# Half of a_u by seven block products, with the bias chain, the dot products and the softmax factor moved, in a decoder block kernel

## The chip, the cores and the metric

The kernel runs on one core of a Trainium2 chip, as one launch. The time is device microseconds of that core: 792.88 us in the median of three runs (792.55 to 793.46). The traces are those of one profiled execution.

## The reference

One decoder layer over x of 512 tokens x 1024 channels, in float32, then a final RMSNorm. Cut to what the change touches:

```
h   = rms_norm(x, norm1_g) * (1 + scale1) + shift1      # shifts, scales, gates: silu(c) @ w_ada + b_ada
z   = h @ w_in        # a_u 1024 | a_v 1024 | q 1024 | k 256 | v 256 | qi 512 | ki 64 | wi 8 | g_a 1024 | g_b 1024
v'  = layer_norm(gelu(a_v), gmlp_ln_g, gmlp_ln_b)       # in 4 chunks of 128 positions and 8 groups of 128 channels
y_a = gelu(a_u) * (einsum('gts,nsgc->ntgc', tril(w_s), v') + b_s)
score  = sum over 8 indexer heads of wi * relu(qi . ki / 8), causal; each query keeps its 128 best keys
y_b    = softmax attention (8 heads of 128, 2 key heads, partial rotary) over the kept keys
merged = sigmoid(g_a) * (y_a @ w_proj_a) + sigmoid(g_b) * (y_b @ w_proj_b)
x = x + gate1 * (merged @ w_out);  x = x + gate2 * swiglu_ffn(rms_norm(x) modulated)
```

Each of the six modulation sections (1024 values) is 8 dot products of 128 rows of the transposed `w_ada` with silu(c).

## The kernel before

Every product with more than float32r precision is made of three matmuls: the weights and the activations are each split into a float32r high part `hi` and the remainder `lo`, and hi*hi, hi*lo and lo*hi are added in PSUM (`mm3`, lines 65 to 68). The order of all instructions is written out by hand; each engine runs its own in program order and waits only on data and on buffers that come free.

**The weight stream.** All weights and most rows of `w_ada` come in one list, `stream`, in fixed order. An entry is 512 KB: a weight chunk ("w") or one dot product ("m"). `issue` (line 91) allocates its raw buffer and puts its load on SyncE's queue. `prep` (line 118) uses it up: a weight chunk gets its `hi` on ScalarE (line 134) and its `lo` on VectorE or GpSimd (line 138); a dot product is one VectorE instruction over the whole 128x1024 raw tile (line 209). A chunk is asked for by `get(i, ahead=2)`, which prepares the stream, in order, up to the weight chunk two behind; before each preparation it issues what has room. The plain raw buffers are three (`RAWB = 3`, line 73):

```
    def room(i):
        ...
        return sum(p["kind"] == "w" or not (p["early"] or p["mid"]) for p in pend) < RAWB
```

Here `pend` is what lies between the entry to be prepared next and entry i. Dot products that are marked "mid" have a tile of their own instead (a tag such as "acc" or "A2") and do not count. `group` (line 231) adds a group of 256 output columns as two chunks of four 128-row blocks, with `nm` dot products behind each chunk.

**The stages around the change.** Indexer and query projections come first, then a_v in eight chunks (steps `vs` 0 to 7, tasks in `VT`), beside which the indexer's scores are built (`idx_mm`, `idx_acc`). Then a_u: four groups, two chunks each (`opt_b`, steps 0 to 7 of `au_tasks` and `au_post`), each chunk 24 matmuls of 512 columns, and behind each chunk a dot product through the tile "acc". In the same steps run the layer norm of v', the spatial mixing (`mix_mm(m)` and `mix_ev(m)` at the steps of `AT`), the bias (`rs_mm`: two matmuls with a tile of ones give the row sums of the masked `w_s`; `bias_mix`: eight VectorE instructions), and the top-k search over the scores, two VectorE passes per round, at the counts of `BG`. Then gate A in two rounds of 512 columns (`xround`, line 1095), each followed by two groups of `w_proj_a` (steps to 29).

**Seven products.** `xround` computes a 512x512 block of columns as a 2x2 block product with seven products instead of eight. One product is 24 matmuls of 256 columns. Sums of weight blocks are formed in DRAM by copying and adding transfers on GpSimd's queue (`x_moves`, eight transfers per round, issued one by one by `x_move`); sums of the activations (`h_sum`, `h_hi`, `h_lo`) are made once and kept.

**Attention with gate B.** `for s in range(NU + 3)` (line 1260) runs 16 attention units in steps; one unit is 128 queries of two heads. Step s does, in this order: the product with v of unit s-3 (`at_pv`) and its evacuation; the scores of unit s (`at_qk`) and their masked maximum on VectorE (`at_soft_a`); the transposes of unit s-2 with `th` on ScalarE and `tl` on VectorE; the softmax factor of unit s-1 (`at_soft_b`, VectorE); the query split of unit s+2 (`qh` ScalarE, `ql` VectorE); the exponentials of unit s (`at_exp`, ScalarE); and `gb_part`, one or two of the 32 pieces of gate B (12 matmuls of 512 columns a pair of column tiles), by

```
    GBN = [1, 2, 2, 1, 1, 1, 2, 2, 2, 2, 2, 2, 2, 2, 2, 2, 2, 2, 0]
```

`gb_part` calls `get` for its chunk, with ahead 1 in step 0 and 2 from then on, so step 1 prepares the stream up to the first chunk of gate B's group 1, and step 2 up to the second. Behind each of gate B's eight chunks stands one dot product, in a plain raw buffer (`nm=1, mraw=False`, line 284). The `lo` of group 1's first chunk is on VectorE, that of its second on GpSimd.

Of the kernel before, what the change touches and what calls it, by code (L numbers as in the profile page):

```python
# [28 lines left out]
def block_kernel(ctx: ExitStack, tc: tile.TileContext, x, x_t, c_row, positions, w_ada_t, w_first, w_in, w_blocks,  # L29
                 gmlp_w_s, gmlp_b_s, w_proj_a, w_proj_b,  # L30
# [868 lines left out]
    def mask_ws():  # L899
        P.affine_select(late["wmT"], late["wmT"], pattern=[[0, 8], [1, 128]], compare_op=OP.is_ge, fill=0.0, base=0,  # L900
                        channel_multiplier=-1)
        late["ones"] = mid.tile([128, 2, 128], F32, name="ones2", tag="ql", bufs=2)[:, 0]
        P.memset(late["ones"], 1.0)

    VT = {0: [load_ws, lambda: rows_a(1), lambda: rows_b(1)],
          1: [lambda: h_hi("S1"), lambda: h_hi("S4"), lambda: h_lo("S1"), lambda: h_lo("S4")],
          2: [lambda: rows_a(2), lambda: rows_b(2), lambda: h_hi("S3")],
          3: [lambda: h_lo("S3")],
          5: [mask_ws],
          7: [load_bs]}  # L910
# [72 lines left out]
    def rs_mm():  # L983
        late["rs"] = [bank(5 + k, "rs") for k in range(2)]
        for k, p in enumerate(late["rs"]):
            T.matmul(p, late["ones"], late["wmT"][:, 4 * k:4 * k + 4].rearrange("p a n -> p (a n)"), start=True, stop=True)

    def bias_mix():
        for m in range(8):
            b = late["bsb"][:, m]  # L990
            V.scalar_tensor_tensor(b, late["rs"][m // 4][:, 128 * (m % 4):128 * (m % 4) + 128], lnbc[:, m:m + 1], b,
                                   op0=OP.mult, op1=OP.add)
# [1092 lines left out]
```

## Time and profile before

| | |
|---|---|
| median of 3 runs | 792.88 us (792.55 to 793.46) |
| the profiled execution | 791.98 us, of which the span of the trace is 790.0 us |
| busy, TensorE matmul | 778.3 us (99%), 4747 matmuls |
| busy, VectorE | 663.7 us (84%) |
| busy, ScalarE | 443.2 us (56%) |
| busy, GpSimd | 181.4 us (23%) |
| mean granted TensorE clock | 0.999 of full speed |

Busy times are shares of the span; ends of matmuls are modelled, so matmuls overlap in the list and the distance from start to start is what one costs. "Idle before" is the time an engine stood still ahead of an instruction, with what released it.

### The profile page before, as it was taken

What the parts mean: (1) busy time and instruction counts of PE and PEld (TensorE: products, weight loads), DVE (VectorE), ACT (ScalarE), POOL (GpSimd) and SP (SyncE); (2) the same over time, 40 slices, a digit from 0 to 9 for tenths busy, and PEclk for the clock granted to TensorE, in tenths of its full rate; (3) what the DMA queues carried; (4) which work ended last, traced back from release to release, by engine and by line L of the source; (5) the groups of instructions that cost most, each with busy time, mean ns of one, the idle gap of its engine ahead of it and who ended that gap; (6) DMA issues with size and microseconds to landing.
All of it is one profiled execution on the core that took longest, in us unless ns stands there. A gap on an engine that the chain in (4) does not pass through costs nothing.

```text
span 790.0 us, 12600 instructions
## 1 busy us (share of the span) xinstructions
PE 778.3 (99%) x4747; PEld 694.5 (88%) x4747; DVE 663.7 (84%) x1114; ACT 443.2 (56%) x777; POOL 181.4 (23%) x220
## 2 busy tenths in 40 slices
PE   8999999999999999999999999999999999999996
PEld 6779988878988988988888899999999999878885
DVE  5988887688897799886787879889999888898777
ACT  6556455443362636666536577555665566576654
POOL 2064234574353501000010000313121322100001
PEclk9999999999999999999999999999999999999999
DMA  9959454789763733148692503989998968666664
GB/s 361 416 156 242 119 146 122 217 231 243 212 215 107 235 112 107 54 135 278 232 234 56 187 1 107 255 251 268 258 259 222 260 201 212 177 200 209 209 192 147
DMA packets 89887, 155.05 MB, mean 196 GB/s; under 512 B 7010, under 2 KB 54770, under 8 KB 89635
## 3 DMA queue, kind: packets, MB, share of 16 engines
q1 hardware_dynamic: 72976, 116.05, 44.6%
q0 software_dynamic: 15952, 37.17, 20.9%
q10 hardware_dynamic: 898, 1.04, 0.4%
q8 instruction: 37, 0.61, 0.3%
q14 instruction: 24, 0.19, 0.1%
HBM read 150.16 MB, written 33.56 MB: 233 GB/s over the span
## 4 chain that ended last, share of the span: by engine, by line
PE 64%; DVE 17%; DMA 9%; ACT 5%; issue 4%; POOL 0%; SPq 0%; POOLq 0%; ACTq 0%; DVEq 0%
PE R L66 5%; PE R L68 5%; PE R L67 5%; PE pb L66 5%; PE pb L67 5%; PE pb L68 5%; DMA mraw<-in_w_ada_t_dram 3%; DMA raw<-in_w_ffn_in_dram 3%; DMA raw<-in_w_ffn_out_dram 3%; PE pfo L67 2%; PE pfo L68 2%; PE pfo L66 2%; PE pav L66 2%; PE pav L67 2%; PE pav L68 2%
## 5 line engine op out<-in xcount | busy, mean ns | idle before, releaser
L134 ACT ACTIVATE hi<-raw 128x1024 fp32r<-128x1024 f32 (+1 forms) x111 | 114.5, 1032 | 81.6 <-PE pb L67 32.4
L138 DVE TENSOR_TENSOR lo<-raw,hi 128x1024 fp32r<-128x1024 f32 (+2 forms) x77 | 90.3, 1174 | 26.9 <-ACT hi L134 26.0
L138 POOL TENSOR_TENSOR lo<-raw,hi 128x1024 fp32r<-128x1024 f32 x27 | 69.5, 2577 | 100.2 <-ACT hi L134 69.6
L67 PE MATMUL pfo<-lo,za 128*128 128x512 f32 (+1 forms) x144 | 55.5, 386 | 0.2 <-DVE lo L138 0.2
L66 PE MATMUL pfo<-hi,za 128*128 128x512 f32 (+1 forms) x144 | 55.5, 385 | 0.0
L68 PE MATMUL pfo<-hi,za 128*128 128x512 f32 (+1 forms) x144 | 55.3, 384 | 0.0
L209 DVE CUSTOM_DVE_ANT_0 mraw<-mraw,scb,cols 128x1024 f32<-128x1024 f32 x24 | 37.6, 1568 | 11.7 <-DMA mraw<-in_w_ada_t_dram 11.7
L66 PE MATMUL R<-tb,sx 128*128 128x256 f32 x160 | 45.0, 281 | 0.3 <-ACT gr L462 0.3
L67 PE MATMUL R<-tb,sx 128*128 128x256 f32 x160 | 44.3, 277 | 0.0
L68 PE MATMUL R<-tb,sx 128*128 128x256 f32 x160 | 44.3, 277 | 0.0
L68 PE MATMUL R<-tb,lo 128*128 128x256 f32 x160 | 44.2, 277 | 0.0
L67 PE MATMUL R<-tb,hi 128*128 128x256 f32 x160 | 44.2, 276 | 0.0
L66 PE MATMUL R<-tb,hi 128*128 128x256 f32 x160 | 44.2, 276 | 0.0
L66 PE MATMUL pb<-h,hi 128*128 128x512 f32 (+1 forms) x112 | 42.7, 382 | 0.0
L68 PE MATMUL pb<-h,lo 128*128 128x512 f32 (+1 forms) x112 | 41.9, 374 | 0.0
L67 PE MATMUL pb<-h,hi 128*128 128x512 f32 (+1 forms) x112 | 41.9, 374 | 0.0
L351 POOL COPY sm<-sm 128x1 f32<-128x1 f32 x36 | 23.2, 644 | 78.7 <-ACT sm L350 78.7
L331 POOL DMA_DIRECT2D wsum<-in_w_ffn_out_dram x24 | 21.2, 885 | 78.0 <-DMA wsum<-wsum 46.1
L66 PEld LDWEIGHTS pfo<-hi,za 128*128 128x128 f32 x144 | 27.1, 188 | 6.1 <-ACT ps L1925 0.6
L67 PEld LDWEIGHTS pfo<-lo,za 128*128 128x128 f32 x144 | 27.1, 188 | 6.1 <-DVE lo L138 0.9
L68 PEld LDWEIGHTS pfo<-hi,za 128*128 128x128 f32 x144 | 27.1, 188 | 5.2
L66 PEld LDWEIGHTS R<-tb,sx 128*128 128x128 f32 x160 | 30.1, 188 | 0.9 <-ACT gr L462 0.5
(398 smaller groups left out, 2697.0 us busy)
## 6 DMA issues: line engine op xcount, KB each, us to landing
raw<-in_w_ffn_in_dram SPq DMA_DIRECT2D x44, 512.0 KB, 5.7
raw<-in_w_in_dram SPq DMA_DIRECT2D x30, 512.0 KB, 3.8
wsum<-in_w_ffn_out_dram POOLq DMA_DIRECT2D x30, 512.0 KB, 8.3
mraw<-in_w_ada_t_dram SPq DMA_DIRECT2D x24, 512.0 KB, 6.3
raw<-wsum SPq DMA_DIRECT2D x20, 512.0 KB, 3.8
s<-in_w_ada_t_dram SPq DMA_DIRECT2D x16, 512.0 KB, 8.8
raw<-in_w_ffn_out_dram SPq DMA_DIRECT2D x16, 512.0 KB, 4.6
xsum<-in_w_blocks_dram POOLq DMA_DIRECT2D x12, 512.0 KB, 6.3
```

Source lines behind the costliest of these rows:

```text
L66: T.matmul(o, wh, rh, start=start, stop=False, **kw)
L67: T.matmul(o, wh, rlo, start=False, stop=False, **kw)
L68: T.matmul(o, wlo, rh, start=False, stop=stop, **kw)
L134: A.activation(hi[:, :m], e["raw"][:, :m], AF.Copy)
L138: e["lo"].tensor_sub(lo[:, :m], e["raw"][:, :m], f(hi[:, :m]))
L209: V.tensor_tensor_reduce(out=raw[:, o], in0=raw[:, o], in1=c, scale=1.0, scalar=col if o.start else bias, op0=OP.mult, op1=OP.add, accum_o ...
L331: P.dma_start(wsum[n][o], src, accum_op=OP.add)
L351: P.tensor_copy(t, t)
```

## The change

- **a_u.** Only its first two groups (512 columns) are left in `opt_b`; the other 512 columns become round 0 of `xround`, ahead of gate A's rounds, with the gelu as evacuation. The host lays out four more blocks of `w_in`.
- **Transfers.** `x_moves` for three rounds, 24 transfers instead of 16, in an order that interleaves the rounds, one in every a_v chunk and at listed steps of a_u.
- **Bias.** The row sums come from a second copy of `w_s` in the other layout: loaded and masked on GpSimd in a_v steps 1 and 2, summed by eight ScalarE copies in step 4, transposed on TensorE and written out in step 6, read back broadcast in step 7; in step 0 of a_u ScalarE scales them in eight copies, and an adding transfer on GpSimd puts `b_s` on top. `rs_mm`, `bias_mix` and the tile of ones are gone. The clearing of the indexer's score tiles moves to the start of a_v.
- **Dot products.** The eight of a_u go to gate B, which then has 16, in plain raw buffers: (2, 3), (3, 2), (2, 2), (1, 1) behind the chunks of its four groups.
- **Softmax factor.** On ScalarE, two scaled copies, in the place where VectorE multiplied; the reciprocal stays on VectorE and comes directly behind `at_soft_a`.
- **Steps.** `au_tasks` has 33 steps instead of 30; `AT`, `BG`, `k_b` and the first query splits move with them.

```diff
-    W_AU = [group(w_in, 256 * g, pool=2, mods=mm_, mraw="acc") for g in range(4)]
-    xsum = {(r, n): dram.tile([128, 1024], F32, name=f"xsum{r}{n}") for r in range(2) for n in (1, 2, 3, 4)}
+    W_AU = [group(w_in, 256 * g, pool=2) for g in range(2)]
+    xsum = {(r, n): dram.tile([128, 1024], F32, name=f"xsum{r}{n}") for r in range(3) for n in (1, 2, 3, 4)}
...
-    xm = [fn for r in range(2) for fn in x_moves(r)]
+    xq = [list(x_moves(r)) for r in range(3)]
+    xm = [xq[r][n] for r, n in ((0, 0), (0, 1), (0, 2), (0, 3), (1, 0), (0, 4), (1, 1), (0, 5), (1, 2), (0, 6), (1, 3), (0, 7),
+                                (1, 4), (2, 0), (1, 5), (2, 1), (1, 6), (2, 2), (1, 7), (2, 3), (2, 4), (2, 5), (2, 6), (2, 7))]
...
-    for r in range(2):
+    for r in range(3):
...
-    W_GB = [group(w_in, 5192 + 256 * g, pool=2 * (g == 1), mods=mm_, nm=1, mraw=False)
+    W_GB = [group(w_in, 5192 + 256 * g, pool=2 * (g == 1), mods=mm_, nm=((2, 3), (3, 2), (2, 2), (1, 1))[g], mraw=False)
...
-        if h == 0:
-            P.memset(sco[i], 0.0)
...
+    def load_wn():
+        late["wn"] = mid.tile([128, 8, 128], F32, name="wn", tag="A1", bufs=1)
+        P.dma_start(late["wn"], gmlp_w_n)
+
+    def mask_wn():
+        P.affine_select(late["wn"], late["wn"], pattern=[[0, 8], [-1, 128]], compare_op=OP.is_ge, fill=0.0, base=0,
+                        channel_multiplier=1)
+
+    def row_sums():
+        for g in range(8):
+            w = late["wn"][:, g]
+            A.activation(w, w, AF.Copy, accum_out=sm[:, g:g + 1])
+
+    def rs_out():
+        p = bank(4 + ibank[0] % 4, "rsT")
+        ibank[0] += 1
+        T.transpose(p[:8, :128], sm[:, 0:8], ident)
+        gr = tiny.tile([128, 128], F32, name="gr", tag="gr", bufs=1)
+        A.activation(gr[:8], p[:8, :128], AF.Copy)
+        A.dma_start(rsd, gr[:8])
+
+    def rs_in():
         late["bsb"] = mid.tile([128, 8, 128], F32, name="bsb", tag="A3", bufs=1)
-        P.dma_start(late["bsb"], bass.AP(tensor=gmlp_b_s.tensor, offset=gmlp_b_s.offset,
-                                         ap=[[0, 128], [128, 8], [1, 128]]))
+        P.dma_start(late["bsb"].rearrange("p a n -> p (a n)"), rows_bcast(rsd, D))
+
+    def rs_scale():
+        for m in range(8):
+            b = late["bsb"][:, m]
+            A.activation(b, b, AF.Copy, scale=lnbc[:, m:m + 1])
+
+    def add_bs():
+        P.dma_start(late["bsb"].rearrange("p a n -> p (a n)"), rows_bcast(gmlp_b_s, D), accum_op=OP.add)
...
+    def clear():
+        for i in (3, 2, 1):
+            P.memset(sco[i], 0.0)
+
+    VT = {0: [clear, load_ws, lambda: rows_a(1), lambda: rows_b(1)],
+          1: [load_wn, lambda: h_hi("S1"), lambda: h_hi("S4"), lambda: h_lo("S1"), lambda: h_lo("S4")],
+          2: [lambda: rows_a(2), lambda: rows_b(2), lambda: h_hi("S3"), mask_wn],
           3: [lambda: h_lo("S3")],
+          4: [row_sums],
           5: [mask_ws],
-          7: [load_bs]}
+          7: [rs_in]}
...
-            if vs % 2:
-                x_move()
+            x_move()
...
+            if vs == 6:
+                rs_out()
...
-    AT = {3: [0], 4: [1, 2], 5: [3], 6: [4], 7: [5], 8: [6], 9: [7]}
+    AT = {2: [0], 3: [1], 4: [2], 5: [3], 9: [6], 10: [7], 11: [4], 12: [5]}
...
-        if s == 2:
-            rs_mm()
...
+            rs_scale()
+            add_bs()
...
-        if s < 9:
+        if s in (0, 1, 2, 3, 4, 6, 7, 9, 10, 12, 15, 18, 20):
...
-    BG = {1: 2, 2: 2, 3: 2, 4: 2, 5: 1, 6: 1, 12: 1, 13: 1, 14: 1, 15: 2, 16: 1, 17: 2, 18: 1,
-          19: 1, 20: 1, 21: 1, 22: 1, 23: 1, 24: 1, 25: 1, 26: 3, 27: 2, 28: 2, 29: 2}
+        if s in (31, 32):
+            at_split(s - 31)
+
+    BG = {1: 3, 2: 3, 3: 3, 6: 1, 7: 1, 8: 1, 9: 1, 14: 1, 15: 1, 16: 1, 17: 1, 18: 1, 19: 1, 20: 2, 21: 1,
+          22: 1, 23: 1, 24: 1, 25: 1, 26: 1, 27: 1, 28: 1, 29: 2, 30: 2, 31: 2}
+    assert sum(BG.values()) == 35
...
-    for g in range(4):
+    for g in range(2):
...
-        xround(r, ga_evac(r))
-        for g in (2 * r, 2 * r + 1):
+    for r in range(3):
+        xround(r, x_evac(sig, 4 * r - 4, AF.Sigmoid, "sg") if r else x_evac(ub, 4, AF.Gelu_apprx_tanh, "u"))
...
-        V.reciprocal(mx[:, 6:8], mx[:, 4:6])
         for e in range(2):
-            V.tensor_scalar(pt[e][:, :n], pt[e][:, :n], mx[:, 6 + e:7 + e], None, op0=OP.mult)
+            A.activation(pt[e][:, :n], pt[e][:, :n], AF.Copy, scale=mx[:, 6 + e:7 + e])
...
+        if 1 <= s <= NU:
+            mx = AS["p", s - 1][1]
+            V.reciprocal(mx[:, 6:8], mx[:, 4:6])
```

## Rows read from the trace of the kernel before

**Rows 1.** Page, part 1: busy us (share of the span) and instructions.

```profile
PE 778.3 (99%) x4747; PEld 694.5 (88%) x4747; DVE 663.7 (84%) x1114; ACT 443.2 (56%) x777; POOL 181.4 (23%) x220
```

**Rows 2.** Waits of PE, 30 to 790 us: total, times, longest.

```profile
PE zx L1116 <- DVE zx L1126: 0.4, 1, 0.4
```

**Rows 3.** Table of one stretch: busy of PE, PEld, DVE, ACT, POOL; clock, DMA, GB/s.

```profile
300.00:320.00 20.00, 19.89 (x129) 18.00 (x128) 18.41 (x50) 14.16 (x35) 3.38 (x1) 1.00 0.34 106
```

**Rows 4.** Timeline, attention: start us, us, engine, line, out<-in [idle before <-releaser].

```profile
301.83 1.28 DVE L1274 TENSOR_TENSOR tl<-pT,th 128x512 fp32r<-128x512 f32 x2
...
303.12 0.28 PE L66 MATMUL pv<-th,v_hi 128*128 128x256 f32 x1
...
308.17 0.28 PE L66 MATMUL pv<-th,v_hi 128*128 128x256 f32 x1
```

**Rows 5.** Timeline of PE: first and last of 21 matmuls; starts of two products.

```profile
194.65 0.39 PE L66 MATMUL pb<-h,hi 128*128 128x512 f32 x1
...
199.18 0.39 PE L68 MATMUL pb<-h,lo 128*128 128x512 f32 x1
...
216.83 0.28 PE L1116 MATMUL zx<-h,hi 128*128 128x256 f32 x1
...
219.55 0.28 PE L1116 MATMUL zx<-hs,hi 128*128 128x256 f32 x1
```

**Rows 6.** Timeline of PE: the row sums and the second matmul behind them.

```profile
172.27 1.88 PE L986 MATMUL rs<-wmT,ones 128*128 128x512 f32 x4
...
174.22 0.40 PE L67 MATMUL pb<-h,hi 128*128 128x512 f32 x1
```

**Rows 7.** Groups of ACT by form, 285 to 375 us: busy, mean ns | idle before.

```profile
L1273 ACT ACTIVATE th<-pT 128x512 fp32r<-128x512 f32 x16 | 9.1, 597 | 10.6 <-PE pT L1216 9.8 <-DVE lo L138 0.8
L1263 ACT ACTIVATE yb<-pv 128x256 fp32r<-128x256 f32 x16 | 6.1, 384 | 11.7 <-PE pv L68 11.5
...
L1193 ACT ACTIVATE pt<-pt,mx 128x512 f32<-128x512 f32 x8 | 5.7, 717 | 1.0 <-DVE mx L1185 1.0
...
L1067 ACT ACTIVATE qh<-qf 128x256 fp32r<-128x256 f32 x10 | 4.2, 417 | 4.0 <-PE qk L67 4.0
...
L1193 ACT ACTIVATE pt<-pt,mx 128x128 f32<-128x128 f32 x8 | 3.2, 395 | 1.8 <-DVE mx L1185 1.8
```

**Rows 8.** DMA issues, 90 to 230 us: count, KB each, median us to landing.

```profile
bsb<-in_gmlp_b_s_dram POOLq DMA_DIRECT2D x1, 512.0 KB, 5.1
```

**Rows 9.** Timelines of POOL and ACT, end of a_v and start of a_u.

```profile
150.95 0.60 POOL L892 DMA_DIRECT2D bsb<-in_gmlp_b_s_dram  x1 [1.76 <-PE idx L743]
...
159.85 2.83 POOL L138 TENSOR_TENSOR lo<-raw,hi 128x1024 fp32r<-128x1024 f32 x1
...
166.35 1.28 ACT L1047 ACTIVATE u<-pb 128x512 f32<-128x512 f32 x2 [3.60 <-PE pb L68]
```

**Rows 10.** Timeline of SP's queue in steps 1 and 2 of attention.

```profile
299.28 0.37 SPq L115 DMA_DIRECT2D raw<-in_w_in_dram  x1
300.53 0.34 SPq L205 DMA_DIRECT2D raw<-in_w_ada_t_dram  x1
```

**Rows 11.** Timeline of DVE in steps 1 and 2 of attention.

```profile
296.83 0.88 DVE L1202 TENSOR_SCALAR pt<-pt,mx 128x512 f32<-128x512 f32 x2
297.63 0.42 DVE L1069 TENSOR_TENSOR ql<-qf,qh 128x256 fp32r<-128x256 f32 x1
297.97 1.28 DVE L209 CUSTOM_DVE_ANT_0 raw<-raw,scb,cols 128x1024 f32<-128x1024 f32 x1
...
299.27 1.23 DVE L138 TENSOR_TENSOR lo<-raw,hi 128x1024 fp32r<-128x1024 f32 x1
...
300.42 0.68 DVE L1183 CUSTOM_DVE_ANT_0 pt<-qk,sco 128x512 f32<-128x512 f32 x1
```

**Rows 12.** DMA issues, 284 to 390 us.

```profile
raw<-in_w_in_dram SPq DMA_DIRECT2D x7, 512.0 KB, 3.7
```

**Rows 13.** Timeline of ACT ahead of attention.

```profile
287.60 1.06 ACT L134 ACTIVATE hi<-raw 128x1024 fp32r<-128x1024 f32 x1 [5.81 <-DMA raw<-in_w_in_dram]
```

More of the change, by code (lines that the diff above doesn't have):

```diff
@@ L29, in block_kernel @@
 def block_kernel(ctx: ExitStack, tc: tile.TileContext, x, x_t, c_row, positions, w_ada_t, w_first, w_in, w_blocks,
-                 gmlp_w_s, gmlp_b_s, w_proj_a, w_proj_b,
+                 gmlp_w_s, gmlp_w_n, gmlp_b_s, w_proj_a, w_proj_b,
                  w_out, w_ffn_in, w_ffn_out, final_norm_g, small, consts, out):
@@ L281, in block_kernel @@
             W_X[r].append(add_w(b, [0, 1, 2, 3], 0, 256, V if p in (2, 5) else P, 48 if p in (1, 4) else 16))
-        for g in (2 * r, 2 * r + 1):
+        for g in (2 * r - 2, 2 * r - 1) if r else ():
             W_PA.append(group(w_pa, 256 * g, mods=mm_, pool=True, nm=(1 - g % 2,) * 2, mraw=("A2", "A3") if g % 2 == 0 else "A2"))
-    W_GB = [group(w_in, 5192 + 256 * g, pool=2 * (g == 1), mods=mm_, nm=1, mraw=False)
+    W_GB = [group(w_in, 5192 + 256 * g, pool=2 * (g == 1), mods=mm_, nm=((2, 3), (3, 2), (2, 2), (1, 1))[g], mraw=False)
             for g in range(4)]
@@ L297, in block_kernel @@
     NZ = 6
+    rsd = dram.tile([8, 128], F32, name="rsd")
     wsum = {n: dram.tile([11 * 128, 512], F32, name=f"wsum{n}") for n in (1, 2, 3, 4)}
@@ L901, in mask_ws @@
                         channel_multiplier=-1)
[L902 to L907, printed above, removed]
+    def clear():
[4 more added lines that the diff above has]
+          2: [lambda: rows_a(2), lambda: rows_b(2), lambda: h_hi("S3"), mask_wn],
           3: [lambda: h_lo("S3")],
+          4: [row_sums],
           5: [mask_ws],
-          7: [load_bs]}
+          7: [rs_in]}
     for _ in range(16):
@@ L981, in mix_ev @@
         ylate.append((austep[0] - 1, hi))
[L983 to L992, printed above, removed]
     ub = {}
     austep = [0, 0]
-    AT = {3: [0], 4: [1, 2], 5: [3], 6: [4], 7: [5], 8: [6], 9: [7]}
+    AT = {2: [0], 3: [1], 4: [2], 5: [3], 9: [6], 10: [7], 11: [4], 12: [5]}
     def au_post():
@@ L1136, in xround, with x_evac @@
             au_post()
-    def ga_evac(r):
+    def x_evac(to, k0, fn, name):
         t = {}
@@ L1143, in ev @@
             if c not in t:
-                t[c] = mid.tile([128, 2, S], F32, name="sg", tag=f"A{c}", bufs=1)
+                t[c] = mid.tile([128, 2, S], F32, name=name, tag=f"A{c}", bufs=1)
                 for m in range(2):
-                    sig[4 * r + 2 * c + m] = t[c][:, m]
-            A.activation(t[c][:, :, 256 * th:256 * th + 256], zb, AF.Sigmoid)
-        return ev
-    for r in range(2):
-        xround(r, ga_evac(r))
-        for g in (2 * r, 2 * r + 1):
+                    to[k0 + 2 * c + m] = t[c][:, m]
+            A.activation(t[c][:, :, 256 * th:256 * th + 256], zb, fn)
+        return ev
+    for r in range(3):
+        xround(r, x_evac(sig, 4 * r - 4, AF.Sigmoid, "sg") if r else x_evac(ub, 4, AF.Gelu_apprx_tanh, "u"))
+        for g in (2 * r - 2, 2 * r - 1) if r else ():
             opt_b(W_PA[g], 8, yT, ((0, 1), (2, 3), (0, 1), (4, 5))[g], pa_evac(g), au_tasks, au_post)
@@ L1267, in block_kernel @@
             at_soft_a(s)
+        if 1 <= s <= NU:
+            mx = AS["p", s - 1][1]
+            V.reciprocal(mx[:, 6:8], mx[:, 4:6])
+        if s < NU:
             if s == 0:
@@ L2026, in block_kernel @@
                 finish(tk)
-_INS = ["x", "x_t", "c_row", "positions", "w_ada_t", "w_first", "w_in", "w_blocks", "gmlp_w_s", "gmlp_b_s",
+_INS = ["x", "x_t", "c_row", "positions", "w_ada_t", "w_first", "w_in", "w_blocks", "gmlp_w_s", "gmlp_w_n", "gmlp_b_s",
         "w_proj_a", "w_proj_b", "w_out", "w_ffn_in", "w_ffn_out", "final_norm_g", "small", "consts"]
@@ L2068 @@
         [w_in[512 * kh:512 * kh + 512, c + 256 * ch:c + 256 * ch + 256].reshape(4, 128, 256).transpose(1, 0, 2)
-         .reshape(128, 1024) for c in (4168, 4680) for kh, ch in ((0, 0), (0, 1), (1, 1), (1, 0))], axis=0)
+         .reshape(128, 1024) for c in (512, 4168, 4680) for kh, ch in ((0, 0), (0, 1), (1, 1), (1, 0))], axis=0)
     given["w_first"] = _np.concatenate([w_in[:, 3072:3328], w_in[:, 2048:2816]], axis=1)
@@ L2072 @@
     given["gmlp_w_s"] = _np.asarray(inputs["gmlp_w_s"])[0].transpose(2, 0, 1)
+    given["gmlp_w_n"] = _np.asarray(inputs["gmlp_w_s"])[0].transpose(1, 0, 2)
     for name in _INS:
```

8 lines of the change are left out of this document (1 added, 7 removed).

## The prediction

> **What bounds the kernel now.** I read the page's busy times first, then the waits of TensorE, then the order of time around the places that the change touches. TensorE is busy for 778.3 of 790.0 us [rows 1]. After the first 30 us the longest single wait of a matmul in the whole trace is 0.4 us [rows 2]. So nothing can be gained but by giving TensorE less to do, and every stall that the change brings in is paid in full, since TensorE has no later idle time in which to win it back.
>
> One stage has no margin: the attention with gate B. From 300 to 320 us VectorE is busy 18.41 of 20 us, and TensorE still 19.89, at a granted clock of 1.00 [rows 3]. The two run in lockstep there: the second `tl` subtraction of attention unit 0 ends at 301.83 + 1.28 = 303.11, and TensorE starts the product that reads it at 303.12 [rows 4]. Whatever delays VectorE or ScalarE in this stage by a microsecond delays TensorE by about as much.
>
> **Seven products for half of a_u.** Two groups of 48 matmuls of 512 columns go. Twenty-one rows lie from 194.65 to 199.18, so one takes 4.53/20 = 0.2265 us and 96 take 21.74. A product of the seven takes 219.55 - 216.83 = 2.72 [rows 5], seven take 19.04. That is -2.7. The existing rounds show one wait of 0.4 for the VectorE addition between their products [rows 2]; the new round may have it too: +0.4. The transfers of its blocks, 24 for 16, are issued on GpSimd, whose order I come to below.
>
> **Bias and row sums.** The two matmuls of row sums and the slow start after them take 174.22 - 172.27 = 1.95, less one normal matmul 1.72 [rows 6]. A transpose takes their place, for which I take no more than a matmul of 512 columns, 0.23 (0.1 to 0.4). That is -1.5. The eight VectorE instructions of the bias go as well, but TensorE did not wait for them, so they count nothing. On ScalarE eight copies with a sum come ahead of the indexer's ReLUs in the fifth a_v chunk; by the 128-column exponential (0.40 each [rows 7]) they take 3.2 us, and the indexer's products, which need the banks that the ReLUs free, may start some tenths late: I take +0.4 (0 to 2). At the start of a_u the chain is longer than before: sums out to memory and broadcast back (a load of that shape landed in 5.1 us [rows 8]), eight scaled copies, an adding transfer on GpSimd, and only behind it the `lo` of a_u's third chunk. Today that `lo` is done at 159.85 + 2.83 = 162.7 and its matmuls start about when the first group ends, 166.35 [rows 9]. The bias load of today is issued at 150.95 [rows 9]; the new broadcast goes out later by the way of the sums to memory, an estimate of 2.6 us (half of the 5.1, for 4 KB), and lands at 158.7. Eight scaled copies at 0.3 to 0.4 end near 161.5, the `hi` and two issues on GpSimd bring the `lo` to about 165.5. That just fits: 0, at worst +2. The interleaving leaves each adding transfer two or three steps behind the one that it adds to, so I expect no wait on GpSimd's queue. The sum up to attention is -2.7 + 0.4 - 1.5 + 0.4 = -3.4 us (-4.3 to 0).
>
> **Dot products in gate B.** Here lies the cost. Eight of the dot products over `w_ada_t` leave a_u, where they had buffers of their own, and gate B gets 16 instead of 8: per weight chunk 2, 3, 3, 2, 2, 2, 1, 1. In gate B they share the three `raw` buffers with the weights, and `ensure` prepares the stream strictly in order, two weight chunks ahead. Step 1 of attention asks for everything up to the first chunk of group 1. Today that is two entries, a dot product and the chunk, and both were loaded in the step before. Then it is four: three dot products and the chunk. Only three can be in flight, all three of them dot products, so the chunk's load can only be issued when the first of the three has been consumed. That this is the rule shows in SyncE's queue: its load of 299.28 goes out at the end of the dot product (297.97 + 1.28), that of 300.53 at the end of the next `lo` [rows 10, 11].
>
> Step 1, worked out. Until 296.8 nothing changes, since VectorE waits for TensorE's scores. Then the softmax factor of unit 0, now two copies on ScalarE, comes ahead of the query split: nothing in the trace shows this copy, so I bound it by VectorE's 0.44 (half of 0.88) and the 0.72 of an exponential of the same width, and take 0.60, the copy `th` of that width [rows 7, 11]. The split then comes at 298.05, and 0.4 later VectorE's low part, at 298.45 to 298.8; today it was done by 297.97 [rows 11]. Three dot products at 1.21 from start to start end at 300.0, 301.2 and 302.45. The chunk's load is issued at 300.05 and lands 3.7 us later [rows 12], 303.75. ScalarE, in order, stands still for it, then makes the `hi` (1.06 [rows 13]) to 304.8; VectorE stands still too, since this chunk's `lo` is its own, and ends it at 305.95 (1.15 of 1.23, as it overlaps). Behind it: the scores of unit 2 (1.41 today, from 300.42 to 301.83 [rows 4, 11]; 1.5 with the reciprocal that is moved ahead), then `tl` of unit 0, first half at 308.15. TensorE starts that product at 308.2 instead of 303.12: +5.1.
>
> Step 2 asks for four entries again: three dot products and the second chunk of group 1. ScalarE scales unit 1 to 308.75 and splits to 309.1, VectorE's low part ends at 309.45, the first dot product at 310.7; only then is the chunk's load issued, which lands at 314.4. ScalarE's `hi` ends at 315.45, and behind it wait the evacuation of the product (0.38 [rows 7]) and `th` of unit 1; VectorE waits for that evacuation, takes the scores of unit 3 to 317.8 and the first half of `tl` to 318.45. TensorE starts the product of unit 1 at 318.5, today at 308.17 [rows 4]: +10.3 in all. Between the two it had 5.0 us of work, so it stands still for about 5.1 us twice.
>
> From step 6 on at most three entries are asked for, and they are in flight before. What stays is the softmax factor: ScalarE gains two copies (1.2 us at 512 columns), VectorE loses 0.88. In the three short steps 3 to 5, about 5 us each, ScalarE has `th` 1.2, factor 1.2, split 0.4, two exponentials 1.4 and more for their sums, and an evacuation 0.4 [rows 7], nearly 5: +0.7. In the later steps VectorE is spared the factor, at most 0.88 a step, and gets a second dot product every other step, 1.21: +0.3 (-0.5 to 2). The stage costs +11.3. Were the landing 2.7 or 5.1 us instead of 3.7, each of the two waits would change by as much: 9.3 to 14.1.
>
> The sum is -3.4 + 11.3 = +7.9. The profiled execution took 791.98 (span 790.0, and 1.98 around it), so 799.9 on its scale; the median of the runs, 792.88, lies 0.9 above it, which gives about 800.8. I say 800.5.
>
> The Trainium skill ("TensorE: Matmul & The Clock Gate", Part 1) says that the array's clock is throttled by default and released by activity, and that an idle stretch lets it fall back to half. In this trace no idle stretch is long enough to show it (0.4 at most, clock 1.00 [rows 2, 3]). By that rule the result would be the third rival below.
>
> **The rivals.** (1) Faster: the fourth entry's transfer is hidden, because ScalarE and VectorE have the time to stand still. What speaks for it: at 287.60 ScalarE had waited 5.81 us for just such a load, and TensorE lost nothing [rows 13]; also VectorE enters the stage a little earlier, its top-k work being done one step sooner. Against it: VectorE is bound by TensorE's scores at that point, so an earlier entry gives no lead, and 303.11 against 303.12 leaves none. Then -3.4 stands, with up to 1.5 lost to the ScalarE copies: 789.5 to 791. It decides if the chunk lands within about 2.4 us of its issue, behind two dot products.
> (2) Half: only one of the two waits is felt, or both in part, so the stage costs 2 to 6 and the whole lands between 791.5 and 797; with about 3.4 the result is no change.
> (3) The throttle: after 5 us without a matmul TensorE resumes at 1.2 GHz. The first fall is partly covered by the second wait; the second is not, and one step of 5.0 us at half speed costs up to 5: +3, about 803.5. For it, that nothing in this kernel has idled so long; against it, that the waits may be shorter than I think.
> (4) GpSimd late in a_u: if the adding transfer or the 24 block transfers hold up a `lo` by more than the step or two that it is ahead, +2 to 4 on top, 803 to 805. For it: the new round takes five `lo` like that of 2.83 us on GpSimd within 19 us [rows 9], and five issues beside them. Against it: today's rounds have the same five, and TensorE's one wait there was not for them [rows 2].
>
> **Chances.** My forecast (797 to 802.5) 0.52; the throttle 0.13; GpSimd late 0.07; half 0.12, one half of it within the bound of no change; faster 0.16. A measurement of this kernel can tell from no change what is over about 0.2%, 1.6 us: faster 0.16, within 0.06, slower 0.78. The range for 8 in 10 goes from 790, which takes in the slow end of the faster case, to 805; the forecast's own range is 797 to 802.5.
>
> **What will show it.** Step by step: block products of a_u at 2.7 us, and no row-sum matmuls; in the attention stage two waits of TensorE of about 5 us each, ahead of the products of units 0 and 1; in SyncE's queue a weight load of group 1 issued only behind a dot product; ScalarE's `hi` of those two chunks released by the DMA after some 4 us; the later steps at their old length. I am wrong if TensorE has no wait over 1 us between 290 and 330, or if those chunks land ahead of the third dot product. If TensorE waits in the a_u stage for a `lo` of GpSimd, the fourth rival holds; if the granted clock falls behind a wait, the third.

## The result, and the profile after

| | before | after |
|---|---|---|
| median of 4 runs, us | 793.17 (792.55 to 794.00) | 803.41 (803.11 to 806.21) |
| profiled execution, us | 791.98 (span 790.0) | 806.21 (span 804.5) |

The changed kernel is slower: ratio 1.0136, 95% [1.0112, 1.0161]. The forecast was 800.5, with 790 to 805 as its range; its own narrower range, 797 to 802.5, was missed by 0.9 us. The profiled execution of after is the longest of its four; the other three have spans of 801.4 to 801.8. So by the two profiles the kernel lost 14.2 us and by the medians 10.2. Stages can only be compared in the profiles, so together they come out about 4 us too dear. Some 1 us of that can be placed, in `w_proj_a` (below). The granted clock doesn't explain the rest: its mean is 0.992 to 0.994 in all four executions.

The starts of the first matmul of each stage show where the time went (differences are taken before rounding):

| stretch | before | after | difference |
|---|---|---|---|
| up to q (untouched) | 61.3 | 61.9 | +0.6 |
| q and a_v, up to a_u | 94.7 | 94.5 | -0.2 |
| a_u and the rounds, up to `w_proj_a` | 72.4 | 67.8 | -4.6 |
| rest up to attention | 63.0 | 64.2 | +1.2 |
| attention with gate B | 81.6 | 98.6 | +17.0 |
| all behind it, to the last matmul | 410.0 | 410.6 | +0.7 |

The page of after answers to [rows 1]: busy times, and two lines of the 40 slices (busy tenths of PE, granted clock in tenths).

```profile
PE 781.2 (97%) x4816; PEld 699.3 (87%) x4816; DVE 659.3 (82%) x1078; ACT 465.6 (58%) x841; POOL 194.2 (24%) x231
...
PE   8999999999999996999999999999999999999996
...
PEclk9999999999999997999999999999999999999999
```

TensorE is no longer busy throughout: the 16th slice (302 to 322 us) has a 6, and its clock a 7. The waits of PE from 30 to 800 us answer to [rows 2], where the longest was 0.4:

```profile
PE pv L67 <- DVE tl L1297: 6.8, 6, 2.5
PE pv L66 <- ACT th L1296: 3.9, 2, 2.0
PE pb L68 <- POOL lo L138: 1.1, 1, 1.1
```

The first two lines hold the two waits forecast for attention units 0 and 1. Each is split into a part before `th` (2.03 and 1.89) and a part before `tl` (2.47 and 1.94), so they are 4.5 and 3.8 us long; the other four waits of the first line, 2.4 us together, come later in the stage. The third line lies ahead of attention, in `w_proj_a`. It comes and goes: of five runs below whose kernels are the same up to attention, e10 has 0.5 us of it, and e1, e3, e5 and e14 have none and take 63.2 us from `w_proj_a` to attention for 64.2. The stretch of [rows 3] and its parts (us, busy of PE, PEld, DVE, ACT, POOL; clock, DMA, GB/s):

```profile
300.00:320.00 20.00, 11.68 (x51) 10.02 (x50) 12.49 (x28) 10.82 (x22) 2.36 (x1) 0.79 0.57 188
...
300.00:305.00 5.00, 0.71 (x3) 0.19 (x1) 3.12 (x8) 2.37 (x4) 0.00 (x0) 0.98 0.80 269
305.00:308.00 3.00, 2.79 (x12) 2.79 (x13) 2.42 (x6) 2.71 (x7) 0.00 (x0) 0.50 0.26 104
308.00:312.00 4.00, 3.74 (x20) 2.78 (x19) 2.37 (x4) 0.30 (x1) 0.00 (x0) 0.98 0.67 206
312.00:316.00 4.00, 0.43 (x2) 0.26 (x2) 2.91 (x9) 2.63 (x5) 2.36 (x1) 0.87 0.51 189
316.00:319.00 3.00, 3.00 (x13) 3.00 (x14) 0.89 (x2) 2.75 (x8) 0.00 (x0) 0.50 0.62 175
319.00:322.00 3.00, 3.00 (x15) 2.88 (x14) 1.79 (x7) 0.61 (x2) 0.00 (x0) 0.53 0.00 0
322.00:325.00 3.00, 3.00 (x23) 2.74 (x21) 1.81 (x3) 2.90 (x8) 0.00 (x0) 1.00 0.00 0
```

TensorE runs 11.68 of 20 us, and after each gap the granted clock is 0.50. Why TensorE stands still, the chain that ended last shows for the same stretch (start, us, what; the longest pieces):

```profile
297.24 3.50 DMA raw<-in_w_in_dram
300.76 1.06 ACT hi L134
301.85 1.23 DVE lo L138
...
304.66 1.33 ACT pt L1221 x2
305.99 0.32 ACT qh L1087
306.33 0.42 DVE ql L1089
306.76 1.20 DVE raw L209
307.99 3.63 DMA raw<-in_w_in_dram
...
315.28 0.60 DVE tl L1297
315.93 0.58 PE pv L67
```

Twice the chain is: a dot product ends on VectorE (`raw`, L209), and only then the weight chunk's load goes out. It lands 3.5 to 3.6 us later, and `hi`, `lo` and `tl` follow. SyncE's queue and VectorE say the same (start, us; the first lines are SP's, as [rows 10]):

```profile
297.24 0.38 SPq L115 DMA_DIRECT2D raw<-in_w_in_dram  x1
...
307.99 0.38 SPq L115 DMA_DIRECT2D raw<-in_w_in_dram  x1
```

```profile
295.93 1.28 DVE L209 CUSTOM_DVE_ANT_0 raw<-raw,scb,cols 128x1024 f32<-128x1024 f32 x1
...
306.67 1.28 DVE L209 CUSTOM_DVE_ANT_0 raw<-raw,scb,cols 128x1024 f32<-128x1024 f32 x1
```

295.93 + 1.28 is 297.21, and 306.67 + 1.28 is 307.95: each load goes out within 0.04 us of the end of the dot product. ScalarE stood still for the landing, as in [rows 13], but now with TensorE behind it:

```profile
300.76 1.06 ACT L134 ACTIVATE hi<-raw 128x1024 fp32r<-128x1024 f32 x1 [3.80 <-DMA raw<-in_w_in_dram]
...
311.70 1.06 ACT L134 ACTIVATE hi<-raw 128x1024 fp32r<-128x1024 f32 x1 [3.99 <-DMA raw<-in_w_in_dram]
```

And in TensorE's timeline, the products of units 0, 1 and 2 (to [rows 4]):

```profile
302.36 0.38 PE L66 MATMUL pv<-th,v_hi 128*128 128x256 f32 x1 [2.03 <-ACT th L1296]
305.21 0.58 PE L67 MATMUL pv<-tl,v_hi 128*128 128x256 f32 x1 [2.47 <-DVE tl L1297]
...
313.63 0.35 PE L66 MATMUL pv<-th,v_hi 128*128 128x256 f32 x1 [1.89 <-ACT th L1296]
315.93 0.58 PE L67 MATMUL pv<-tl,v_hi 128*128 128x256 f32 x1 [1.94 <-DVE tl L1297]
...
323.44 0.28 PE L66 MATMUL pv<-th,v_hi 128*128 128x256 f32 x1
```

Attention begins 2.9 us earlier than before (288.4 for 291.3), so 2.9 is added to set these beside [rows 4]: unit 0 is +5.0 late (305.21 + 2.9 - 303.12), unit 1 +10.7, unit 2 +13.1 (323.44 + 2.9 - 313.25, its start before). From unit 2 to unit 15 the kernel before took 59.3 us, after takes 63.2: another +3.9, spread over the steps.

### The profile page after: what moved, and what is told of

The parts are those of the page before. It is cut to its first block, busy times and chain, and to the rows that moved or that the text cites. A ratio compares the mean times of both kernels' runs of the same rounds, so it can differ in the third digit from the quotient of the medians.

```text
span 804.5 us, 12815 instructions
## 1 busy us (share of the span) xinstructions
PE 781.2 (97%) x4816; PEld 699.3 (87%) x4816; DVE 659.3 (82%) x1078; ACT 465.6 (58%) x841; POOL 194.2 (24%) x231
## 4 chain that ended last, share of the span: by engine, by line
PE 68%; DVE 16%; ACT 8%; DMA 4%; issue 3%; POOL 1%; ACTq 0%; POOLq 0%; DVEq 0%
PE R L66 6%; PE R L68 6%; PE R L67 6%; PE pb L68 5%; PE pb L67 5%; PE pb L66 5%; PE pfo L67 4%; PE pfo L66 3%; PE pfo L68 3%; PE pav L66 2%; PE pav L67 2%; PE pav L68 2%; PE o L553 2%; DVE lo L138 1%; PE o L555 1%
## 5 line engine op out<-in xcount | busy, mean ns | idle before, releaser
L134 ACT ACTIVATE hi<-raw 128x1024 fp32r<-128x1024 f32 (+2 forms) x114 | 117.6, 1032 | 88.2 <-PE pb L67 21.2
L138 DVE TENSOR_TENSOR lo<-raw,hi 128x1024 fp32r<-128x1024 f32 (+2 forms) x79 | 93.8, 1189 | 35.1 <-ACT hi L134 35.0
L138 POOL TENSOR_TENSOR lo<-raw,hi 128x1024 fp32r<-128x1024 f32 x28 | 72.0, 2578 | 93.3 <-ACT hi L134 93.3
L354 POOL COPY sm<-sm 128x1 f32<-128x1 f32 x36 | 27.1, 759 | 79.9 <-ACT sm L353 79.9
L67 PE MATMUL R<-tb,sx 128*128 128x256 f32 x160 | 44.3, 277 | 0.0
L68 PE MATMUL R<-tb,sx 128*128 128x256 f32 x160 | 44.3, 277 | 0.0
L66 PEld LDWEIGHTS R<-tb,sx 128*128 128x128 f32 x160 | 30.1, 188 | 1.1 <-ACT R L1843 0.5
L66 PEld LDWEIGHTS R<-tb,hi 128*128 128x128 f32 x160 | 30.0, 188 | 0.0
L68 PEld LDWEIGHTS R<-tb,sx 128*128 128x128 f32 x160 | 30.0, 188 | 0.0
L67 PEld LDWEIGHTS R<-tb,sx 128*128 128x128 f32 x160 | 30.0, 188 | 0.0
L68 PEld LDWEIGHTS R<-tb,lo 128*128 128x128 f32 x160 | 30.0, 188 | 0.0
```

The lines of the kernel that those rows point to most:

```text
L66: T.matmul(o, wh, rh, start=start, stop=False, **kw)
L67: T.matmul(o, wh, rlo, start=False, stop=False, **kw)
L68: T.matmul(o, wlo, rh, start=False, stop=stop, **kw)
L134: A.activation(hi[:, :m], e["raw"][:, :m], AF.Copy)
L138: e["lo"].tensor_sub(lo[:, :m], e["raw"][:, :m], f(hi[:, :m]))
L354: P.tensor_copy(t, t)
```

## The experiments

The theory: the stage lost its time to (a) the fourth entry of steps 1 and 2, whose load waits for a free `raw` buffer, with the clock at half behind each gap, and (b) the softmax factor on ScalarE. The rivals: (a) does all; (b) does all; or the number of dot products does it, wherever they stand. The table gives each kernel's ratio to the kernel before, run beside it, and from its profile the stage (first score product to first `w_proj_b` product), cut at the products of units 2 and 15.

| kernel | ratio, 95% | to unit 2 | 2 to 15 | stage |
|---|---|---|---|---|
| before | | 21.9 | 59.3 | 81.6 |
| after | 1.0136 [1.0112, 1.0161] | 35.0 | 63.2 | 98.6 |
| e2, before + dot products | 1.0173 [1.0154, 1.0192] | 35.3 | 60.1 | 95.8 |
| e6, before + factor on ScalarE | 1.0061 [1.0039, 1.0082] | 24.3 | 62.1 | 86.7 |
| e7, e6 with the reciprocal first | 0.9992 [0.9982, 1.0002] | 22.1 | 59.4 | 81.9 |
| e3, after, factor on VectorE | 1.0101 [1.0077, 1.0126] | 33.2 | 59.7 | 93.3 |
| e1, after, two per chunk | 1.0062 [1.0041, 1.0083] | 25.3 | 65.4 | 91.0 |
| e5, e1 and e3 together | 0.9992 [0.9976, 1.0009] | 24.3 | 61.4 | 86.0 |
| e10, e1 with the reciprocal first | 1.0006 [0.9994, 1.0017] | 24.0 | 60.8 | 85.2 |
| e14, requests of four late | 1.0089 [1.0071, 1.0107] | 23.3 | 69.8 | 93.5 |
| e15, two in `w_proj_a` | 0.9972 [0.9958, 0.9985] | 22.2 | 60.8 | 83.3 |

**e2: the dot products alone.** The kernel before, with the dot products placed as in the change and nothing else of it.

```diff
-    W_AU = [group(w_in, 256 * g, pool=2, mods=mm_, mraw="acc") for g in range(4)]
+    W_AU = [group(w_in, 256 * g, pool=2) for g in range(4)]
-    W_GB = [group(w_in, 5192 + 256 * g, pool=2 * (g == 1), mods=mm_, nm=1, mraw=False)
+    W_GB = [group(w_in, 5192 + 256 * g, pool=2 * (g == 1), mods=mm_, nm=((2, 3), (3, 2), (2, 2), (1, 1))[g], mraw=False)
```

> The kernel before with only the eight dot products moved from a_u to gate B, in the places of the change; seven products, bias chain and softmax factor as before. Theory: two waits of about 5 us ahead of the products of units 0 and 1, clock down behind them, and VectorE fuller later: 10 to 15 us above before, 803 to 808. Rival (softmax factor): 793 to 797.

805.45 us, ratio 1.0173. The same two waits of PE stand there, each of their parts twice:

```profile
PE pv L67 <- DVE tl L1274: 4.1, 2, 2.2
PE pv L66 <- ACT th L1273: 3.9, 2, 2.1
```

Of its +14.2 in the stage, +13.4 has come by unit 2, and only +0.8 behind it. So the placement alone makes the two waits and loses as much up to unit 2 as after does, but almost nothing of its +3.9 behind. How much of after's own loss up to unit 2 is the placement's is less sure: e3 below has the same requests and the factor on VectorE too, and loses 11.3 us there. 2.0 of the 2.1 us between e2 and e3 arise ahead of unit 0; e2 has a wait of 1.0 us there for the maximum of the scores that e3 doesn't have. So where TensorE waits, a difference of 2 us between two profiles of this stage needn't come from the requests or the factor; the kernels without long waits, before and e7, agree to 0.3.

**e6 and e7: the factor alone.** e6 is the kernel before with the factor on ScalarE, as in the change: the reciprocal is taken behind the maximum over the scores of the next unit (`at_soft_a`). e7 is the same with the reciprocal ahead of it. The diff is e7's; in e6 the three added lines stand behind the last.

```diff
-            V.tensor_scalar(pt[e][:, :n], pt[e][:, :n], mx[:, 6 + e:7 + e], None, op0=OP.mult)
+            A.activation(pt[e][:, :n], pt[e][:, :n], AF.Copy, scale=mx[:, 6 + e:7 + e])
...
+        if 1 <= s <= NU:
+            mx = AS["p", s - 1][1]
+            V.reciprocal(mx[:, 6:8], mx[:, 4:6])
         if s < NU:
             at_qk(s)
             at_soft_a(s)
```

> The kernel before with only the softmax factor moved to ScalarE and the reciprocal moved as in the change. Theory: no wait for a load, VectorE waits some 0.6 us per step for the query split behind the factor but is spared 0.5 to 0.9: 0 to 4 us above before, 793 to 797. Rival (softmax factor): more than 8 above, over 801.

796.19 us, ratio 1.0061.

> The kernel before with the softmax factor on ScalarE, as in the run of the factor alone (0.61% above before), but with the reciprocal ahead of the scores' maximum on VectorE instead of behind it; nothing else. Theory (a closed loop from step to step: maximum, reciprocal, factor on ScalarE, split, exponentials, evacuation, maximum; ScalarE waited 18 us for the reciprocal in 16 steps): the factor leaves the loop, ScalarE makes it while it waited before; the stage falls from 86.7 us to 81 to 83, the time to within 1 us of before, 790.5 to 792.5. Rival (ScalarE has too much work in this stage, wherever the factor stands): stays at 795 to 797.

791.54 us, ratio 0.9992: no difference from the kernel before. The waits of e6 in the stage, then those of e7:

```profile
ACT pt L1201 <- DVE mx L1269: 18.1, 16, 2.2
DVE ql L1069 <- ACT qh L1067: 6.2, 9, 1.7
PE pv L67 <- DVE tl L1277: 3.5, 5, 1.3
```

```profile
DVE ql L1069 <- ACT qh L1067: 1.8, 5, 0.6
ACT pt L1201 <- DVE mx L1266: 1.3, 4, 0.4
```

This settles (b). In e6 ScalarE waits 16 times for the tiny reciprocal, which stands on VectorE behind the maximum of the scores that TensorE has just made. Behind the waiting factor stands the split `qh`, for which VectorE's `ql` waits, and behind `ql` stands the rest of VectorE's step: a loop that closes once a step. Taken first, the reciprocal is long ready (18.1 us of waits become 1.3), and the same two copies cost nothing. After shows the loop as well, with 15 waits for 16:

```profile
ACT pt L1221 <- DVE mx L1289: 18.6, 15, 2.5
...
DVE ql L1089 <- ACT qh L1087: 6.4, 9, 1.7
```

**e3, e1, e5: one part of the change put back, then both.** e3 has the factor on VectorE; e1 has two dot products per weight chunk, so that no step asks for four entries; e5 has both. The first pair of lines is e3's, the second e1's.

```diff
-            A.activation(pt[e][:, :n], pt[e][:, :n], AF.Copy, scale=mx[:, 6 + e:7 + e])
+            V.tensor_scalar(pt[e][:, :n], pt[e][:, :n], mx[:, 6 + e:7 + e], None, op0=OP.mult)
...
-    W_GB = [group(w_in, 5192 + 256 * g, pool=2 * (g == 1), mods=mm_, nm=((2, 3), (3, 2), (2, 2), (1, 1))[g], mraw=False)
+    W_GB = [group(w_in, 5192 + 256 * g, pool=2 * (g == 1), mods=mm_, nm=2, mraw=False)
```

> The changed kernel with the softmax factor back on VectorE (reciprocal where the change has it). Theory: the two waits and the clock stay, VectorE has up to 0.88 us more in each step but no longer waits 0.64 for the query split: 799 to 806. Rival (softmax factor): below 794.

799.81 us, ratio 1.0101. The two gaps stay (33.2 us to unit 2), the later steps are back at 59.7. The stage is 5.3 us shorter than in after, close to the 5.1 that the factor cost alone in e6.

> The changed kernel with gate B's 16 dot products two behind every chunk, so that one request never asks for more than three entries and all of them are in flight before. Theory (two exposed weight loads and the clock that falls behind them): no wait of TensorE over 1 us in attention steps 1 to 4, clock 1.00 there; 803.4 less 10.7 and 2.4 is 790.3, and one to three us more for dot products that now stand in later steps: 791 to 794. Rival (the softmax factor on ScalarE is the main cost): falls by less than 4, 799 to 803. Second rival (sixteen dot products are too much for VectorE in gate B, wherever they stand): also 799 to 803.

796.76 us, ratio 1.0062: less of the loss is gone than was expected. The two gaps of 4.5 and 3.8 us are gone, though waits of 1.2 and 1.9 us remain in their places, against the expectation of none over 1 us. The half clock is gone too (same columns as above):

```profile
300.00:325.00 25.00, 22.30 (x142) 19.79 (x143) 16.92 (x48) 20.41 (x49) 2.39 (x1) 1.00 0.29 91
```

But the factor's loop remains, and costs more with a second dot product in each request (65.4 us from unit 2 to 15, for 62.1 in e6).

> The changed kernel with the dot products spread two behind every chunk and the softmax factor back on VectorE. If the two causes add up, the stage is that of the spread run (91.0 us) less the 5.1 that the factor alone cost: 86; with the 4 us that a_u gains, 0 to 2 us above before: 791 to 793.5. Rival (the second dot product of each pull fills VectorE, and the factor on top of it makes it worse): 795 or more.

791.24 us, ratio 0.9992. The stage is 86.0 against 93.3 in e3, and 91.0 in e1 against 98.6 in after: the four-entry requests cost 7.3 to 7.6 us of stage, with the factor on either engine.

**e10: spread, with the reciprocal first.**

```diff
-        if s < NU:
-            at_qk(s)
-            at_soft_a(s)
...
             V.reciprocal(mx[:, 6:8], mx[:, 4:6])
+        if s < NU:
+            at_qk(s)
+            at_soft_a(s)
```

> The changed kernel with the dot products spread two behind every chunk, the factor on ScalarE, and the reciprocal ahead of the scores' maximum. Theory of the loop: the factor costs nothing then and spares VectorE 0.5 to 0.9 us per step, so part of the second dot product is paid: stage 82 to 86, 788 to 792. Rival (ScalarE's work): as the spread run, 796.

792.64 us, ratio 1.0006: just above what was expected. The stage is 85.2, 5.8 less than e1; 2.1 of the 3.6 that it still has over before lie ahead of unit 2, where both requests now have three entries. So of after's +17.0 the four-entry requests make about 7.5 and the factor about 5. With neither the loop nor such a request, 3.6 (e10) to 4.4 us (e5) are left, and for that part the third rival holds: sixteen dot products cost it even when they are spread. How much of it is their number, and how much the three entries of a request, was not separated.

**e14: the four-entry requests elsewhere.** All 16 dot products stay in gate B, but the crowded requests come at the end, in steps 12 and 14, which are short. The reciprocal is first, as in e10.

```diff
+    W_GB = [group(w_in, 5192 + 256 * g, pool=2 * (g == 1), mods=mm_, nm=((1, 1), (2, 2), (2, 2), (3, 3))[g], mraw=False)
```

> The changed kernel with all 16 dot products in gate B, but the chunks with three behind them are the last two (1, 1, 2, 2, 2, 2, 3, 3), so that the two requests of four entries come in attention steps 12 and 14, where VectorE and ScalarE were half idle; reciprocal ahead of the maximum. Theory (an exposed load holds ScalarE's and VectorE's queues, busy or not): two waits of 2 to 4 us there, 3 to 7 us above the run with two behind every chunk and the same reciprocal (792.6): 795 to 799. Rival (the front of the stage was the trouble, and idle engines hide a load): no wait over 1 us, 789 to 792.

799.05 us, ratio 1.0089. The loss moved with the requests: now 23.3 us to unit 2, and 69.8 behind it. The waits of the stage show both, TensorE's and then ScalarE's for the two loads (3.9 in step 12, 4.9 in step 14, where the chunk is the first of `w_proj_b`):

```profile
PE pv L66 <- DVE mx L1286: 4.5, 2, 2.7
```

```profile
ACT hi L134 <- DMA raw<-in_w_in_dram: 5.0, 2, 3.9
ACT hi L134 <- DMA raw<-in_w_proj_b_dram: 4.9, 1, 4.9
```

Here too the load goes out as a dot product ends (350.18 + 1.28 = 351.46, the load at 351.50). So the loss goes with the request's size against the three buffers, not with its place in the stage. A kernel with a fourth `raw` buffer, the direct proof, was not run.

**e9, e12, e13: dot products back in a_u.** e9 puts eight back (four behind the chunks of the two groups, four in the first round), with one per chunk in gate B and the factor on VectorE; e12 puts four back, with the reciprocal first; e13 is e12's placement with the factor on VectorE. The diff has e12's lines, and last, in the loop over a round's blocks, those that e9 has more (its `nm` is 1).

```diff
+    W_AU = [group(w_in, 256 * g, pool=2, mods=mm_, mraw="acc") for g in range(2)]
+    W_GB = [group(w_in, 5192 + 256 * g, pool=2 * (g == 1), mods=mm_, nm=((1, 1), (1, 1), (2, 2), (2, 2))[g], mraw=False)
...
+            if r == 0 and p in (0, 1, 3, 5):
+                add_m(*next(mm_), mid="acc")
```

> The changed kernel with its eight dot products back in a_u, through the tile of their own (four behind the chunks of the two groups, four in the new round), gate B with one behind each chunk as before, and the softmax factor on VectorE. Theory: the attention stage is that of before, 81 to 83 us, and a_u keeps its gain of 3 to 4.5: 787 to 789. Rival (dot products in the new round delay its splits or transfers, so that a_u's gain depends on their leaving): a_u's gain is gone, 790 to 793.

> The changed kernel with four of its eight dot products back in a_u (behind the four chunks of the two groups, whose steps are 5.4 us long), the other four in gate B behind the chunks of its last two groups, where VectorE was half idle, and the reciprocal ahead of the maximum. Theory: no request asks for more than three entries, no dot product is added to the full steps 1 to 6, ScalarE's factor is off the loop: stage 81 to 83, a_u keeps 3.5 to 4: 787.5 to 789.5, 0.4 to 0.6% below before. Rival (a_u's gain needs all eight gone): a_u gains less than 2, 790 or more.

> The same, with the softmax factor on VectorE and the reciprocal where the change has it. Theory: as the run with the factor on ScalarE to within 1 us, since neither place is on the loop then: 787.5 to 790.

All three missed: 805.73 (1.0155 [1.0118, 1.0192]), 794.17 (1.0028 [1.0010, 1.0046]) and 798.04 us (1.0063 [1.0039, 1.0086]). The attention stage of e9 and e12 did as expected (81.5 and 82.3 us), but the stretch from the first round to `w_proj_a`, 44.3 us in after, took 61.1, 50.8 and 52.3. The gain of the seven products was lost there; of the rivals, that of e12 fits. In e12, TensorE's wait and, ahead of it, ScalarE's:

```profile
PE zx L1136 <- ACT zk L1127: 3.4, 1, 3.4
...
ACT zk L1127 <- DVE y L1013: 7.8, 2, 5.9
```

The `y` are late by 8.1 us, mainly because VectorE's first dot product there took 7.66 us instead of 1.28 (VectorE's timeline of e12, then GpSimd's):

```profile
160.76 7.66 DVE L209 CUSTOM_DVE_ANT_0 mraw<-mraw,scb,cols 128x1024 f32<-128x1024 f32 x1 [1.30 <-DMA mraw<-in_w_ada_t_dram]
...
181.95 0.75 DVE L1006 SCALAR_TENSOR_TENSOR y<-mix,cols,bsb 128x512 f32<-128x512 f32 x1
```

```profile
161.13 3.18 POOL L138 TENSOR_TENSOR lo<-raw,hi 128x1024 fp32r<-128x1024 f32 x1
...
164.17 3.16 POOL L138 TENSOR_TENSOR lo<-raw,hi 128x1024 fp32r<-128x1024 f32 x1
```

In after, without that dot product, the first `y` starts at 173.84, here at 181.95. That the collision is the whole loss was not isolated: two more dot products stand ahead of that `y`, and VectorE waited for the loads of all three. The chain from the late `y` to TensorE's wait of 3.4 is what the rows show.

e13's stage missed as well: 85.8 us, 3.5 above e12's, where within 1 was expected. Its loss comes in the last steps, and no request there has more than three entries. The load of step 14's chunk went out at 360.96, some 5 us before ScalarE was free for it, but landed only 8.2 us after its issue:

```profile
369.17 1.06 ACT L134 ACTIVATE hi<-raw 128x1024 fp32r<-128x1024 f32 x1 [3.13 <-DMA raw<-in_w_proj_b_dram]
```

So a request that fits the buffers can still wait when its transfer is slow. The DMA engines were busy for 0.95 of the time from 362 to 366; what slowed this load was not isolated.

**e15: the version that follows.** The reciprocal first; in gate B 2, 1, 1, 2 and then two per chunk, so that no request has four entries; the two dot products left over stand behind the second group of `w_proj_a`.

```diff
-            W_PA.append(group(w_pa, 256 * g, mods=mm_, pool=True, nm=(1 - g % 2,) * 2, mraw=("A2", "A3") if g % 2 == 0 else "A2"))
+            W_PA.append(group(w_pa, 256 * g, mods=mm_, pool=True, nm=(1, 1) if g == 1 else (1 - g % 2,) * 2, mraw=("A2", "A3") if g % 2 == 0 else "A2"))
...
+    W_GB = [group(w_in, 5192 + 256 * g, pool=2 * (g == 1), mods=mm_, nm=((2, 1), (1, 2), (2, 2), (2, 2))[g], mraw=False)
```

> The changed kernel with the reciprocal ahead of the maximum and gate B's dot products at (2, 1), (1, 2), (2, 2), (2, 2); the two that are left over stand behind the chunks of the second group of w_proj_a, where VectorE was busy 7.3 of 11 us, through a tile of their own. In the run with two behind every chunk the stage lost 2.1 us against before in its first two requests and about 1 after. Theory: steps 1 and 2 ask for two entries again, as before the change, so the 2.1 come back: stage about 83, 789.5 to 791.5, 0.1 to 0.3% below before. Rival (a dot product in w_proj_a's steps delays something there, as it did in a_u): 792 or more.

789.76 us, ratio 0.9972 [0.9958, 0.9985]: faster than both kernels, and than before by 0.28%. Its longest wait of TensorE in attention is 0.5 us:

```profile
PE pv L67 <- DVE tl L1297: 0.8, 2, 0.5
```

## Why the prediction was right, and where it was short

**Up to attention, -3.4 forecast; -2.9 measured.** Of this, +0.6 arose ahead of all that was changed, so the change itself gave -3.5. Its parts differ: the stretch of a_u gained 4.6 where the terms made 3.8, the ScalarE sums in a_v cost nothing (forecast +0.4), and 1.1 was lost to a `lo` of GpSimd in `w_proj_a`, a small case of the fourth rival in a stage that the prediction did not look at, and one that four kernels equal to this one up to attention don't show. In a_u itself that rival did not come true.

**Step 1 and step 2: right in place and mechanism, and nearly in size.** On the clock of before the forecast had the chunk's loads issued at 300.05 and 310.7; measured, with 2.9 added, 300.14 and 310.89. Landing 3.50 and 3.63 for 3.7. Units 0 and 1 were +5.0 and +10.7 late for +5.1 and +10.3. (The prediction read 303.12 as the matmul that waits for `tl`; that row reads `th`, and the one that reads `tl` follows 0.11 us behind.) TensorE itself waited less than the 5.1 us twice, 4.5 and 3.8, because its work between the two ran in part at half the clock; the path that set unit 1's start was that of the load, on VectorE and ScalarE. e2 reproduces the waits alone, e1 takes most of them away, e14 moves them. The rivals "faster" and "half" fall with the first.

**The clock: the third rival, given 0.13, came true as an addition to the forecast.** Both gaps were followed by a granted clock of 0.50. The first fall (305 to 308) lies beneath the second load's wait, as that rival said; the second (316 to 322) is on the path: unit 1 to unit 2 took 323.44 - 315.93 = 7.5 us for 5.1, +2.4. The price is not fixed: in e3, behind a like gap, the granted clock was 0.50 from 313.8 to 317 and already 0.96 in the 3 us after, and the same stretch took 6.4. The forecast should have carried the term in its sum, since the same sum had TensorE idle for 5 us twice.

**The failed term: "What stays is the softmax factor: ... +0.7", and "In the later steps ... +0.3".** Together +1.0 was forecast behind unit 2, +3.9 measured. The price of the two copies was nearly right (two at 512 columns took 1.33 for 1.20). What failed is that only busy times were added up, with ScalarE thought free to start. It had to wait in every step for the reciprocal, which the change puts behind the score maximum on VectorE; e6 shows it alone (+2.8 behind unit 2), e7 takes it away. The prediction counted this reciprocal as 0.1 us of VectorE and did not ask what queues behind the instruction that waits for it.

The stage thus was forecast at +11.3 and measured at +17.0: 2.4 of the difference is the clock, 2.9 what came behind unit 2, nearly all of it the factor's loop (e2 has 0.8 there without it), and 0.4 the waits. The medians, +10.2 for +7.6, show less than half of that miss; most of the rest is in the profiled execution alone, and its stage can't be told. That 803.41 lies within 790 to 805 owes something to the width of that range: two terms were missing or far too small, and the narrower range that went with the mechanism was missed.

**Dot products out of a_u: counted at nothing, worth more.** In e9, e12 and e13, with four or eight of them back, a_u and the rounds take 84.5, 74.3 and 75.7 us, for 67.8 in after and 72.4 in before. So the third round's gain hangs on their leaving; why is shown only for the first part of e12's chain. The prediction charged the move with its cost in gate B alone.

## What to carry to other kernels

Count, for every request of an in-order stream, the entries it asks for against the buffers it shares: here one more than the buffers put a landing of 3.5 to 3.6 us on the path of every engine that works through the queue in order, and spreading the same work (e1, e15) took most or all of it away. Where work moves from a full engine to a free one, ask what its operand waits for and what stands behind it: 0.88 us a unit taken off VectorE cost 5.1 us of stage (e6) until a 0.16 us reciprocal was moved ahead of a reduction that it did not need.
